# Mixing tiles beside the last convolution, and the first pair's blocks summed in other tiles

## The chip, the cores and the metric

The kernel runs on one core of one Trainium2 chip. The time is the device time of one execution in microseconds (us): the median of three runs. The profile is one further execution, recorded by the hardware profiler. A core has five engines with a queue of instructions each: PE (TensorE, matrix products; PEld is its loading of weights), DVE (VectorE), ACT (ScalarE), POOL (GpSimd) and SP (SyncE, which only starts transfers). Engines wait for one another by semaphores, and a wait holds everything behind it in the same queue. Results of PE stand in PSUM banks until ACT or DVE has read them.

## The reference

One layer over 128 context tokens and 512 latent tokens, model width 1024. One wide projection feeds two branches, a gated long convolution and an attention over a neighbourhood:

```python
h = x * (1 + scale) + shift
z = h @ w_in          # 4 x hyena, 4 x attention, 2 x mixing, 1024 columns each
v_h, x1, x0 = short_conv(z_hyena)
u = v_h * x1
y_h = (irfft(rfft(u) * rfft(filter)) + u * d_bias) * x0
y_a = neighbourhood_attention(q, k, v, cached k and v, bias)     # 16 heads
p_h = (y_h * silu(g_h)) @ w_bh
p_a = (y_a * silu(g_a)) @ w_ba
m_h, m_a = split(sigmoid(m))
x_new = layer_norm(ALPHA * x + gate * ((m_h * p_h + m_a * p_a) @ w_out))
```

The keys and values of the context tokens are outputs too. Everything is computed in float32 precision: a weight or a token matrix is split into a high and a low part, and three products (high by high, high by low, low by high) make one.

## The kernel before

**Tiles of the projection.** The 640 tokens lie as columns, in two halves of 320. The weights come from `wall`, a list of 128 x 1024 tiles; tile i makes 128 output channels: 32 to 39 are queries, 40 to 47 keys, 56 to 63 the attention's gates (`T_GA`), 64 to 71 the mixing of the hyena branch (`T_MH`). The tokens stand in `hH`, `hL` (high and low part) and for two of the eight blocks of model channels in `hHp`, `hLp`.

**Direct tiles.** `proj(i)` makes one tile as 8 blocks x 3 passes x 2 halves = 48 matmuls of 128 x 320 into two of the four PSUM banks of `ps_mm`, named mm<i>_0 and mm<i>_1. Its weights come from `wtile`: raw load, high part `wh` on ACT, low part `wl` on DVE, or with "dma" the negated high part to which GpSimd adds `wall` by an accumulating transfer.

**Pairs.** `pair_tile(p)` makes two tiles together with a Strassen-like scheme: seven products of 12 matmuls, so 84 for 96. `ORDER` lists their token operands: b11, b21, b22 are blocks of the tokens, t1 to t4 are sums of blocks, which were stored to DRAM (`tok_d`) and come back as tiles named t1_00 and so on. On the weights' side a pair p needs seven 128 x 512 blocks: a11 and a12 are the halves of the raw tile ra<p>, s3 and a22 those of rb<p>, and s2_<p> is a tile of its own. s2 and s3 have a part of the other tile added by accumulating transfers of GpSimd. `sum1` (DVE) adds s1 = s2 + a22. Each block is split into wb<7p+j> (`high` on ACT, `low` on DVE, four products ahead) and used by product j, whose bank is sp<p>_x. Each half of a product calls `tick()`, which runs what `later(fn, n)` has put off for n ticks: evictions, sums, steps of the attention.

**Stages.** A prologue, then four quarters in which direct tiles, the short convolution and the long convolution by Fourier matrices are woven together. The last quarter's long convolution (`long_conv(3)`, `long_conv_back(3)`) is woven with `hand_over()`, which makes the direct tiles of values 0, queries and keys 0, queries and keys 1. The end of the convolution is a chain over three engines: ACT and DVE split the spectrum (ph3_*, pl3_*), PE multiplies it into yb3_*, ACT evicts it (ye3, yep3), PE transposes it (yp3, y6, y7), DVE multiplies it into yu6 and yu7, and GpSimd stores these to `yu_d`. `first_gates()` then makes the two gate tiles 56 and 57 directly, and converts the first blocks of pair 0. `scratch()` copies half of `hHp`, `hLp` into the first blocks of `hH`, `hL`, in whose second halves nothing is needed any more, so that the old tiles become eviction space (`spare_hHp`, `spare_hLp`). Then come eight heads; `HEADS` gives each its pairs (h gates of the hyena branch, m mixing, a gates of the attention, q queries and keys of a head), and `attend(j)` weaves in the attention of head j: `tiled(i)` makes scores and softmax steps, among them scalings on GpSimd (`scaled`), `turned(i)` the transposes and the product with the values. Last come w_bh, w_ba, w_out and the layer norm.

**What sets the order.** PE, DVE and ACT run in written order in the quarters and the heads:

```python
with tc.manual_schedule(engines={PE, DVE, Activation}):     # written out at line 1351
    for _ in first_gates():
```

SP and GpSimd are ordered by a scheduler, except for loads pinned by `pinned[0]`. Tiles are taken from pools: a new tile waits for the last use of the one in its slot. `yhp` has 9 rows named "yh", in which x0 of the convolution, yu6, yu7 and some token sums stand.

Of the kernel before, what the change touches and what calls it, by code (L numbers as in the profile page):

```python
# [45 lines left out]
def tile_hyena_natten_step(ctx: ExitStack, tc: tile.TileContext, a, o):  # L46
# [802 lines left out]
    def hand_over():  # L849
# [6 lines left out]
        out["slots_r"] = left.enter_context(tc.tile_pool(name="slots_r", bufs=1))  # L856
        yield from queries(1)
        last_keys = keys(1)
        yield next(last_keys)
        wraw(T_GA)  # L860
        wraw(T_GA + 1)
        yield from last_keys
        early[T_GA] = wtile(T_GA, "dma")

    def first_gates():
        early[T_GA + 1] = wtile(T_GA + 1)
        yield from gate_a(0)
        for g in range(AHEAD - 1):
            if g == 1:
                sum1(0)  # L870
            high(g)
            low(g)
        yield from gate_a(1)
# [242 lines left out]
    def operand(name):  # L1116
# [3 lines left out]
        if name == "b11":  # L1120
# [13 lines left out]
    def load_pair(p):  # L1134
        if p < len(pairs):
            load_a(p)
            load_b(p)
# [3 lines left out]
    def load_b(p):  # L1141
        i0, i1 = pairs[p]
        wall = a["wall"]
        ra = raws.pop(("a", p))
        rb = sp.tile([P, 1024], F32, tag="rb", bufs=2, name=f"rb{p}")
        s2 = sp.tile([P, 512], F32, tag="s", bufs=3, name=f"s2_{p}")[:]
        load_to(rb[:], wall[i1])
        load_to(s2, wall[i0][:, :512])
        a11, a12, s3, a22 = (r[:, 512 * h : 512 * h + 512] for r in (ra, rb) for h in range(2))
        nc.gpsimd.dma_start(s2, wall[i1][:, :512], accum_op=ALU.add)  # L1150
        nc.gpsimd.dma_start(s3, wall[i1][:, 512:], accum_op=ALU.add)  # L1151
        sums_[p] = [a11, None, s2, s3, a12, a22, None]
# [36 lines left out]
    def pair_tile(p, use):  # L1189
# [16 lines left out]
        for j in range(7):  # L1206
# [3 lines left out]
            dst, x = ps["xyvzxvz"[j]], operand(ORDER[j])  # L1210
# [72 lines left out]
    HEADS = ("h0 m0", "q2 h1 m1", "q3 m2 a2", "q4 h2 m3", "q5 m4 a4", "q6 h3 m5", "q7 a6", "m6 m7")  # L1283
# [13 lines left out]
    raws["a", 0] = slot(1, "v", "ra0")  # L1297
    load_to(raws["a", 0][:, :1024], a["wall"][pairs[0][0]])
    load_b(0)
    load_sums(1, SUMS[:2])  # L1300
    biases[0] = [bias_tile(h) for h in range(2)]
    load_sums(1, SUMS[2:3])
    load_sums(0, SUMS[3:])
    load_sums(1, SUMS[3:])
    pinned[0] = True
    load_pair(1)
# [44 lines left out]
    with tc.manual_schedule(engines={mybir.EngineType.PE, mybir.EngineType.DVE, mybir.EngineType.Activation}):  # L1351
        for _ in first_gates():
            pass
        scratch()
        for j in range(8):
            side, n_main, n_side = attend(j), N_PAIR * len(HEADS[j].split()), N_ATT if j < 7 else N_ATT + 3
            done = taken = 0
            for _ in mains(j):
                done += 1
                while taken * n_main < done * n_side:  # L1360
# [308 lines left out]
```

## Time and profile before

| | |
|---|---|
| median of 3 runs | 916.91 us (916.83 to 917.48) |
| profiled execution, its own time | 916.55 us |
| its span from first to last instruction | 914.8 us |
| granted TensorE clock, mean | 0.982 |
| PE busy | 877.8 us, 96% |
| DVE, ACT, POOL busy | 636.2, 449.5 and 186.0 us |
| moved by DMA | 168.56 MB |

The profile names an instruction by engine, line, operation and its tiles (out<-in). A releaser behind "<-" is what ended the idle time before it, by the semaphores. Times in the text are microseconds from the start of the span. The conversion of the weights for mm57 begins at 356.5, and the first transposes of attention inside pair 1 at 417.3: between these lies what the change rewrites.

### The profile page before, as it was taken

To read this page: it belongs to the slowest core of one execution; us is meant where nothing else is said; L and a number is where in the kernel's file an instruction comes from. 1 tells how busy PE (TensorE), PEld (TensorE's weight loads), DVE (VectorE), ACT (ScalarE), POOL (GpSimd) and SP (SyncE) were. 2 spreads that over 40 slices of the span, in tenths; PEclk is the share of its full clock that TensorE was granted. 3 is DMA by queue.
4 is the path that set the end of the run, shared out by engine and by line. 5 is a ranking of instruction groups with operands and counts; after the bars stand their busy time and mean duration, and the time that the engine had idled before them with its cause. 6 is when DMAs were issued, how large, how long until landed. Compare 5 with 4: busy or idle time off the path is not lost. (4 is left out here: it accounts for less than half of the span.)

```text
span 914.8 us, 17154 instructions
## 1 busy us (share of the span) xinstructions
PE 877.8 (96%) x6476; PEld 846.3 (93%) x6476; DVE 636.2 (70%) x1216; ACT 449.5 (49%) x955; POOL 186.0 (20%) x215
## 2 busy tenths in 40 slices
PE   8999999999899999669999999999999999999995
PEld 7799999999899999559999999999999999999884
DVE  4896675993785656628777677868777577667566
ACT  4485555645555443416666565656566632233200
POOL 0020111211100100144444334333435200000000
PEclk9999999999999999888999999999999999999998
DMA  8975676876556762896676767676654576446232
GB/s 335 403 194 133 144 169 149 222 174 155 123 115 161 193 158 50 281 311 202 166 224 175 205 165 218 179 209 163 197 148 122 183 276 236 170 149 212 101 110 89
DMA packets 72367, 168.56 MB, mean 184 GB/s; under 512 B 10684, under 2 KB 28860, under 8 KB 72285
## 3 DMA queue, kind: packets, MB, share of 16 engines
q1 hardware_dynamic: 53180, 123.06, 40.2%
q0 software_dynamic: 13488, 38.80, 21.9%
q10 hardware_dynamic: 5616, 5.61, 1.8%
q8 instruction: 51, 0.84, 0.4%
q14 instruction: 32, 0.25, 0.1%
HBM read 142.80 MB, written 23.99 MB: 182 GB/s over the span
## 5 line engine op out<-in xcount | busy, mean ns | idle before, releaser
L1214 PE MATMUL sp<-t,wb 128*128 128x320 f32 x1008 | 160.3, 313 | 0.2
L1214 PEld LDWEIGHTS sp<-t,wb 128*128 128x128 f32 x1008 | 151.9, 190 | 0.9 <-issue 0.9
L1214 PE MATMUL sp<-hH,wb 128*128 128x320 f32 x504 | 124.6, 318 | 10.5 <-DVE spare_hHp L1202 6.9
L1214 PEld LDWEIGHTS sp<-hH,wb 128*128 128x128 f32 x504 | 88.7, 192 | 13.7 <-ACT wb L1167 7.1
L182 PE MATMUL mm<-hH,wh 128*128 128x320 f32 x336 | 85.0, 318 | 10.9 <-DVE kl L836 5.5
L182 PE MATMUL mm<-hL,wh 128*128 128x320 f32 x336 | 83.1, 316 | 0.4 <-DVE hL L329 0.4
L182 PE MATMUL mm<-hH,wl 128*128 128x320 f32 x336 | 82.6, 315 | 0.2 <-DVE wl L102 0.2
L1214 PE MATMUL sp<-hL,wb 128*128 128x320 f32 x252 | 79.5, 315 | 0.6 <-DMA hL<-hLp 0.6
L162 POOL DMA_DIRECT2D wl<-wall x33 | 28.8, 872 | 226.9 <-ACT wl L161 208.0
L182 PEld LDWEIGHTS mm<-hH,wh 128*128 128x128 f32 x336 | 58.3, 192 | 13.6 <-DVE kl L836 6.1
L1167 ACT ACTIVATE wb<-s 128x512 fp32r<-128x512 f32 x63 | 39.8, 632 | 54.6 <-DVE s L1157 23.2
L163 ACT ACTIVATE wh<-raw 128x1024 fp32r<-128x1024 f32 x33 | 35.1, 1064 | 59.6 <-PE mm L182 44.5
L1175 DVE TENSOR_TENSOR wb<-s,wb 128x512 fp32r<-128x512 f32 x63 | 44.9, 714 | 25.9 <-ACT wb L1167 25.7
L182 PEld LDWEIGHTS mm<-hL,wh 128*128 128x128 f32 x336 | 58.3, 192 | 1.5 <-DVE hL L329 1.2
L182 PEld LDWEIGHTS mm<-hH,wl 128*128 128x128 f32 x336 | 58.5, 193 | 0.9 <-DVE wl L102 0.6
L994 POOL TENSOR_SCALAR p<-p,sm 128x384 f32<-128x384 f32 x32 | 47.1, 1481 | 31.7 <-DVE sm L992 17.5
L994 POOL TENSOR_SCALAR edge<-edge,sm 128x320 f32<-128x320 f32 x32 | 38.0, 1196 | 69.9 <-DVE sm L992 69.9
L1214 PEld LDWEIGHTS sp<-hL,wb 128*128 128x128 f32 x252 | 48.5, 192 | 1.1 <-DMA hL<-hLp 1.0
L1488 PE MATMUL out<-woh,yhs 128*128 128x512 f32 (+1 forms) x176 | 45.7, 373 | 0.0
L182 PE MATMUL mm<-yhs,wh 128*128 128x320 f32 x224 | 42.0, 309 | 0.0
L1151 POOL DMA_DIRECT2D rb<-wall x21 | 18.4, 875 | 107.0 <-DMA rb<-wall 87.1
L1202 DVE TENSOR_TENSOR spare_hHp<-sp,yu 128x320 f32<-128x320 f32 x63 | 30.3, 482 | 11.5 <-PE sp L1214 11.0
(404 smaller groups left out, 2260.6 us busy)
## 6 DMA issues: line engine op xcount, KB each, us to landing
raw<-wall SPq DMA_DIRECT2D x54, 512.0 KB, 3.7
wl<-wall POOLq DMA_DIRECT2D x33, 512.0 KB, 6.2
rb<-wall SPq DMA_DIRECT2D x21, 512.0 KB, 4.9
ra<-wall SPq DMA_DIRECT2D x21, 512.0 KB, 4.0
ada<-wada SPq DMA_DIRECT2D x16, 512.0 KB, 7.5
tm<-bias SPq DMA_DIRECT2D x16, 512.0 KB, 7.7
s<-wall SPq DMA_DIRECT2D x21, 256.0 KB, 4.1
rb<-wall POOLq DMA_DIRECT2D x21, 256.0 KB, 4.1
```

Source lines behind the costliest of these rows:

```text
L162: nc.gpsimd.dma_start(wl, a["wall"][i], accum_op=ALU.add)
L163: nc.scalar.activation(wh, raw[:], AF.Copy)
L182: nc.tensor.matmul(ps[hf][:, :HALF], wt[k], x[:, hf * HALF : (hf + 1) * HALF], start=(i == 0 and k == 0), stop=(i == lead[2] and k == NK - ...
L994: nc.gpsimd.tensor_scalar_mul(pv, pv, sm[:, 2, c : c + 1])
L1151: nc.gpsimd.dma_start(s3, wall[i1][:, 512:], accum_op=ALU.add)
L1167: nc.scalar.activation(made[g][:, 0], sums_[g // 7][g % 7], AF.Copy)
L1175: nc.vector.tensor_tensor(made[g][:, 1], sums_[g // 7][g % 7], f(made[g][:, 0]), op=ALU.subtract)
L1202: nc.vector.tensor_tensor(c, dst, c if j == 3 else ps["u"], op=ALU.add)
L1214: nc.tensor.matmul(dst, wk, x(xi, k), start=j < 4 and k == 0 and i == 0, stop=k == 3 and i == 2, skip_group_check=True,)
L1488: ins = nc.tensor.matmul(dst, m[k][:, c0 : c0 + P], w[:, c : c + n], start=(first and k == 0), stop=(last and k == 5), skip_group_check=True,)
```

## The change

1. In `hand_over()` the direct tiles of head 1's queries and keys go out. In their place `mix_tile(0)` and `mix_tile(1)` make mixing tiles 64 and 65 directly: 48 matmuls each, two halves of tanh on ACT into a row of `yhp` (mx0, mx1), one store by SP to `mh_d`.
2. Pair 0 was the gate pair h0 and pair 1 the mixing pair m0. Now pair 0 is q1, head 1's queries and keys, pair 1 is h0, and there is no m0. The number of pairs and of direct tiles is the same.
3. Pair 0 reads block b11 from the four token tiles where they are (`operand(name, p)`); from pair 1 on it is read from the copy that `scratch()` makes.
4. `first_blocks()` loads and sums pair 0's blocks in other tiles, earlier in the program: rb0 in two tiles of the pool `slots_q`, s2_0 in a row of `yhp`.
5. The load of rb is split in two halves for every pair, and the accumulating transfers of later pairs are put off by five ticks, or, for pair 1, written ahead of the heads.
6. The low part of gate tile 57's weights is made by "dma".
7. GpSimd and SP run in written order in the heads as well.
8. In head 0 the attention is put back by 8 of the 28 steps of its pairs.
9. The pool `slots_r` is opened after the hand-over, and the loads of sums, biases and pair 1 are written in another order.

On PE, around the end of the last convolution, the rows before were these (mm56 and mm57 are the gate tiles):

```order
L172 MATMUL yb3_1_3965<-ph3_3_3976,dftL_102 128x256
L182 MATMUL mm56_0_4360<-hH_85,wl56_4309 128x320
L182 MATMUL mm56_1_4361<-hH_85,wl56_4309 128x320
L170 MATMUL yb3_2_3999<-ph3_4_4000,dftH_101 128x256
L171 MATMUL yb3_2_3999<-pl3_4_4001,dftH_101 128x256
L172 MATMUL yb3_2_3999<-ph3_4_4000,dftL_102 128x256
L170 MATMUL yb3_2_3999<-ph3_4_4000,dftH_101 128x256
L171 MATMUL yb3_2_3999<-pl3_4_4001,dftH_101 128x256
L172 MATMUL yb3_2_3999<-ph3_4_4000,dftL_102 128x256
L625 MATMUL yp3_4033<-pack2_380,yep3_3924 128x128 x2
L635 MATMUL y6_4038<-pack2_380,ye3_3923 128x128 x4
L635 MATMUL y7_4072<-pack2_380,ye3_3923 128x128 x4
```

And now, where the same transposes end:

```order
L170 MATMUL yb3_2_3999<-ph3_4_4000,dftH_101 128x256
L171 MATMUL yb3_2_3999<-pl3_4_4001,dftH_101 128x256
L172 MATMUL yb3_2_3999<-ph3_4_4000,dftL_102 128x256
L170 MATMUL yb3_2_3999<-ph3_4_4000,dftH_101 128x256
L171 MATMUL yb3_2_3999<-pl3_4_4001,dftH_101 128x256
L172 MATMUL yb3_2_3999<-ph3_4_4000,dftL_102 128x256
L625 MATMUL yp3_4033<-pack2_380,yep3_3924 128x128 x2
L635 MATMUL y6_4038<-pack2_380,ye3_3923 128x128 x4
L635 MATMUL y7_4072<-pack2_380,ye3_3923 128x128 x4
L182 MATMUL mm56_0_4340<-hH_85,wh56_4283 128x320
L182 MATMUL mm56_1_4341<-hH_85,wh56_4283 128x320
L182 MATMUL mm56_0_4340<-hL_87,wh56_4283 128x320
```

The convolution's matmuls stood inside mm56, and behind the transposes came mm57; now all thirty of them and the transposes stand in one block between the last matmul of mixing tile 65 and the first of mm56.

ACT evicts these banks. Before, at the same place (k1 and kp1 are head 1's keys, sg0 the first gate):

```order
L621 ACTIVATE ye3_3923<-yb3_0_3925 128x512
L101 ACTIVATE ph3_4_4000<-X3_3531 128x512
L621 ACTIVATE ye3_3923<-yb3_1_3965 128x512
L621 ACTIVATE yep3_3924<-yb3_2_3999 128x256
L826 ACTIVATE k1_4290<-mm41_0_4236 128x64
L826 ACTIVATE k1_4290<-mm41_0_4236 128x128 x2
L829 ACTIVATE kp1_4295<-mm41_0_4236 128x128
L832 ACTIVATE k1_4290<-ck1_4227 128x2x128
L826 ACTIVATE k1_4290<-mm41_1_4237 128x64
L826 ACTIVATE k1_4290<-mm41_1_4237 128x2x128
L499 ACT_TABLE_LOAD
L499 ACTIVATE sg0_4359<-mm56_0_4360 128x320
```

Now (mx0 and mx1 are the rows of the mixing tiles):

```order
L101 ACTIVATE ph3_3_3976<-W3_3705 128x512
L101 ACTIVATE ph3_4_4000<-X3_3531 128x512
L621 ACTIVATE ye3_3923<-yb3_1_3965 128x512
L621 ACTIVATE yep3_3924<-yb3_2_3999 128x256
L870 ACT_TABLE_LOAD
L870 ACTIVATE mx0_4157<-mm64_0_4165 128x320
L870 ACTIVATE mx0_4157<-mm64_1_4166 128x320
L870 ACTIVATE mx1_4218<-mm65_0_4226 128x320
L870 ACTIVATE mx1_4218<-mm65_1_4227 128x320
L499 ACTIVATE sg0_4339<-mm56_0_4340 128x320
```

The evictions of the key tile mm41 behind the convolution are replaced by those of both mixing tiles, and mx0's row is the one that x0 of yu7 has just left.

On GpSimd, behind the memsets of the attention's edge tiles, before (edge, p0 and pp0 are scaled scores of attention):

```order
L900 MEMSET edge31_4113 128x64
L994 ISA
L994 TENSOR_SCALAR edge00_4107<-edge00_4107,sm0_4525 128x320
L994 TENSOR_SCALAR edge01_4109<-edge01_4109,sm0_4525 128x320
L994 TENSOR_SCALAR p0_0_1_4526<-p0_0_1_4526,sm0_4525 128x384
L994 TENSOR_SCALAR p0_1_1_4527<-p0_1_1_4527,sm0_4525 128x384
L996 TENSOR_SCALAR pp0_4528<-pp0_4528,sm0_4525 128x128 x2
L1151 DMA rb1_4347<-wall 128x512
L1150 DMA s2_1_4348<-wall 128x512
L1151 DMA rb2_4615<-wall 128x512
L1150 DMA s2_2_4616<-wall 128x512
```

And now:

```order
L908 MEMSET edge31_4113 128x64
L1167 DMA s2_1_4317<-wall 128x512
L1168 DMA rb1_4316<-wall 128x512
L1167 DMA s2_0_4295<-wall 128x512
L1167 DMA s2_2_4546<-wall 128x512
L1168 DMA rb2_4545<-wall 128x512
L1002 ISA
L1002 TENSOR_SCALAR edge00_4107<-edge00_4107,sm0_4583 128x320
L1002 TENSOR_SCALAR edge01_4109<-edge01_4109,sm0_4583 128x320
L1002 TENSOR_SCALAR p0_0_1_4584<-p0_0_1_4584,sm0_4583 128x384
L1002 TENSOR_SCALAR p0_1_1_4585<-p0_1_1_4585,sm0_4583 128x384
L1004 TENSOR_SCALAR pp0_4586<-pp0_4586,sm0_4583 128x128 x2
```

The accumulating transfers of pairs 1 and 2 stood behind the scalings and now stand ahead of them, together with that of pair 0's s2.

On SP, near the mixing stores, now:

```order
L871 DMA mh_d_77<-mx0_4157 128x640
L63 DMA t3_10_4310<-tok_d_81 128x640
L63 DMA t3_11_4312<-tok_d_81 128x640
L63 DMA ra1_4314<-wall 128x1024
L871 DMA mh_d_77<-mx1_4218 128x640
L63 DMA rb1_4316<-wall 128x512 x2
L63 DMA s2_1_4317<-wall 128x512
L63 DMA s2_0_4295<-wall 128x512
L63 DMA t1_10_4321<-tok_d_81 128x640
```

The load of pair 0's s2_0 stands behind the stores of both mixing rows and behind the loads of pair 1's blocks; before, it stood ahead of the token sums t2.

```diff
--- before.py
+++ after.py
@@ -853,17 +853,25 @@
         out["slots_l"] = left.enter_context(tc.tile_pool(name="slots_l", bufs=1))
         out["slots_q"] = left.enter_context(tc.tile_pool(name="slots_q", bufs=1))
         yield from chain(values(0), queries(0), keys(0))
-        out["slots_r"] = left.enter_context(tc.tile_pool(name="slots_r", bufs=1))
-        yield from queries(1)
-        last_keys = keys(1)
-        yield next(last_keys)
-        wraw(T_GA)
-        wraw(T_GA + 1)
-        yield from last_keys
-        early[T_GA] = wtile(T_GA, "dma")
+        yield from mix_tile(0)
+        last_mix = mix_tile(1)
+        yield next(last_mix)
+        for i in range(2):
+            wraw(T_GA + i)
+        yield from last_mix
+        for i in range(2):
+            early[T_GA + i] = wtile(T_GA + i, "dma")
+        load_a(0)
+        first_blocks()
+
+    def mix_tile(n):
+        th = row(yhp, "yh", f"mx{n}")
+        for hf, p in enumerate((yield from proj(T_MH + n, eng="dma"))):
+            nc.scalar.activation(th[:, CS[hf]], p[:, :HALF], AF.Tanh, scale=0.5)
+        nc.sync.dma_start(mh_d[n], th[:])
+        yield
 
     def first_gates():
-        early[T_GA + 1] = wtile(T_GA + 1)
         yield from gate_a(0)
         for g in range(AHEAD - 1):
             if g == 1:
@@ -1113,11 +1121,11 @@
         yield
 
 
-    def operand(name):
+    def operand(name, p):
         if name in tok:
             return lambda i, k: tok[name][i][k // 2][:, HALF * (k % 2) : HALF * (k % 2) + HALF]
         i0, j = int(name[1]) - 1, int(name[2]) - 1
-        if name == "b11":
+        if name == "b11" and p:
             return lambda i, k: (hH, hL)[i][:, k % 2, CS[k // 2]]
         return lambda i, k: (hH, hL)[i][:, 4 * i0 + k, CS[j]]
 
@@ -1134,22 +1142,32 @@
     def load_pair(p):
         if p < len(pairs):
             load_a(p)
-            load_b(p)
+            later(load_b(p), 5)
         else:
             wraw(T_BH + p - len(pairs))
 
     def load_b(p):
-        i0, i1 = pairs[p]
-        wall = a["wall"]
-        ra = raws.pop(("a", p))
         rb = sp.tile([P, 1024], F32, tag="rb", bufs=2, name=f"rb{p}")
         s2 = sp.tile([P, 512], F32, tag="s", bufs=3, name=f"s2_{p}")[:]
-        load_to(rb[:], wall[i1])
-        load_to(s2, wall[i0][:, :512])
-        a11, a12, s3, a22 = (r[:, 512 * h : 512 * h + 512] for r in (ra, rb) for h in range(2))
-        nc.gpsimd.dma_start(s2, wall[i1][:, :512], accum_op=ALU.add)
-        nc.gpsimd.dma_start(s3, wall[i1][:, 512:], accum_op=ALU.add)
-        sums_[p] = [a11, None, s2, s3, a12, a22, None]
+        return blocks(p, s2, rb[:, :512], rb[:, 512:])
+
+    def first_blocks():
+        s2 = row(yhp, "yh", "s2_0")[:, :512]
+        blocks(0, s2, *(out["slots_q"].tile([P, NT], F32, tag=t, name=f"rb0_{t}")[:, :512] for t in ("q", "ql")))()
+
+    def blocks(p, s2, s3, a22):
+        w0, w1 = (a["wall"][i] for i in pairs[p])
+        load_to(s3, w1[:, :512])
+        load_to(a22, w1[:, 512:])
+        load_to(s2, w0[:, :512])
+        ra = raws.pop(("a", p))
+        sums_[p] = [ra[:, :512], None, s2, s3, ra[:, 512:], a22, None]
+
+        def summed():
+            nc.gpsimd.dma_start(s2, w1[:, :512], accum_op=ALU.add)
+            nc.gpsimd.dma_start(s3, w1[:, 512:], accum_op=ALU.add)
+
+        return summed
 
     def sum1(p):
         s_ = sums_[p]
@@ -1207,7 +1225,7 @@
             g = 7 * p + j
             if j < 4:
                 ps["xyvz"[j]] = acc(f"sp{p}_{j}")[:, :HALF]
-            dst, x = ps["xyvzxvz"[j]], operand(ORDER[j])
+            dst, x = ps["xyvzxvz"[j]], operand(ORDER[j], p)
             for k in range(4):
                 wh, wl = (made[g][:, i, P * k : P * k + P] for i in range(2))
                 for i, (wk, xi) in enumerate(((wh, 0), (wh, 1), (wl, 0))):
@@ -1280,7 +1298,7 @@
         return pair_tile(p, use)
 
     N_PAIR = 14
-    HEADS = ("h0 m0", "q2 h1 m1", "q3 m2 a2", "q4 h2 m3", "q5 m4 a4", "q6 h3 m5", "q7 a6", "m6 m7")
+    HEADS = ("q1 h0", "q2 h1 m1", "q3 m2 a2", "q4 h2 m3", "q5 m4 a4", "q6 h3 m5", "q7 a6", "m6 m7")
     MAKE = dict(a=gates_a, h=gates_h, q=queries_keys, m=mix)
 
     def tiles_of(item):
@@ -1294,16 +1312,16 @@
     pairs = [tiles_of(item) for item in items]
 
     weave(hand_over(), chain(long_conv(3), long_conv_back(3), attention_setup()), 4 * NK + N_VALUES, N_CONV + N_BACK + 1)
-    raws["a", 0] = slot(1, "v", "ra0")
-    load_to(raws["a", 0][:, :1024], a["wall"][pairs[0][0]])
-    load_b(0)
+    out["slots_r"] = left.enter_context(tc.tile_pool(name="slots_r", bufs=1))
+    pinned[0] = True
     load_sums(1, SUMS[:2])
-    biases[0] = [bias_tile(h) for h in range(2)]
+    load_a(1)
+    sums_of_second = load_b(1)
     load_sums(1, SUMS[2:3])
+    biases[0] = [bias_tile(0)]
     load_sums(0, SUMS[3:])
     load_sums(1, SUMS[3:])
-    pinned[0] = True
-    load_pair(1)
+    biases[0].append(bias_tile(1))
     pinned[0] = False
 
     def yh_home(i):
@@ -1348,16 +1366,19 @@
         for n in (2, 3):
             later(lambda n=n: yh_split(n), 6 + 2 * n)
 
-    with tc.manual_schedule(engines={mybir.EngineType.PE, mybir.EngineType.DVE, mybir.EngineType.Activation}):
+    engines = {getattr(mybir.EngineType, e) for e in ("PE", "DVE", "Activation", "Pool", "SP")}
+    with tc.manual_schedule(engines=engines):
         for _ in first_gates():
             pass
+        sums_of_second()
         scratch()
         for j in range(8):
-            side, n_main, n_side = attend(j), N_PAIR * len(HEADS[j].split()), N_ATT if j < 7 else N_ATT + 3
+            late = 8 if j == 0 else 0
+            side, n_main, n_side = attend(j), N_PAIR * len(HEADS[j].split()), {0: 3, 7: N_ATT + 3}.get(j, N_ATT)
             done = taken = 0
             for _ in mains(j):
                 done += 1
-                while taken * n_main < done * n_side:
+                while taken * (n_main - late) < (done - late) * n_side:
                     if next(side, StopIteration) is StopIteration:
                         break
                     taken += 1
```

## The prediction

> **What bounds the kernel now.** I read the page first: busy shares, then the strip in 40 slices (22.9 us each; PE is TensorE, and the figures are tenths of a slice that it was busy, below them the granted clock).
>
> ```profile
> span 914.8 us, 17154 instructions
> PE 877.8 (96%) x6476; PEld 846.3 (93%) x6476; DVE 636.2 (70%) x1216; ACT 449.5 (49%) x955; POOL 186.0 (20%) x215
> PE   8999999999899999669999999999999999999995
> PEclk9999999999999999888999999999999999999998
> ```
>
> TensorE is the bound nearly everywhere, so only its idle time and a lowered clock can be won. Both are found in one place, slices 17 to 19 (366 to 434 us), and the change rewrites that place. Next I read windows (start:end, length, busy time and count of PE, PEld, DVE, ACT, POOL, then clock, DMA share, GB/s); the first is the whole stretch from the first matmuls of gate tile mm56 to the point in pair 1 behind which nothing is held up any more.
>
> ```profile
> 356.57:417.31 60.74, 43.46 (x258) 40.76 (x257) 26.61 (x64) 21.49 (x53) 13.78 (x20) 0.83 0.75 239
> 365.00:376.00 11.00, 4.84 (x32) 3.83 (x31) 6.67 (x18) 4.18 (x11) 3.29 (x8) 0.87 0.62 185
> 386.00:394.00 8.00, 3.79 (x22) 2.95 (x21) 4.10 (x13) 1.80 (x6) 0.00 (x0) 0.76 1.04 373
> 405.00:412.00 7.00, 0.46 (x4) 0.20 (x2) 1.47 (x3) 0.63 (x1) 2.50 (x3) 0.90 0.95 150
> 440.00:480.00 40.00, 40.00 (x320) 39.00 (x321) 30.63 (x75) 23.57 (x56) 17.97 (x19) 1.00 0.67 190
> 376.00:377.00 1.00, 1.00 (x5) 1.00 (x5) 0.39 (x1) 0.90 (x3) 0.00 (x0) 0.50 0.76 211
> 380.00:381.00 1.00, 1.00 (x9) 1.00 (x8) 0.00 (x0) 0.52 (x1) 0.00 (x0) 1.00 1.12 376
> ```
>
> PE idles 60.74 - 43.46 = 17.3 us here, nearly all in three stalls (11.00 - 4.84 = 6.2 in the second window, then 4.2 and 6.5), and not at all from 440 to 480. After the first stall the clock is 0.50 at 376 and 1.00 at 380; it is a second cost. The list of waits names the releasers (sum, count, longest):
>
> ```profile
> PE mm L182 <- DVE kl L836: 5.5, 2, 5.2
> PE sp L1214 <- DMA hH<-hHp: 3.6, 1, 3.6
> PE sp L1214 <- DVE spare_hHp L1202: 6.9, 1, 6.9
> DVE s L1157 <- DMA s<-wall: 11.2, 1, 11.2
> ```
>
> Stall 1: mm57 needs the PSUM banks of head 1's keys, whose eviction stands behind the end of the long convolution. Stall 2: pair 0's first product reads the scratch copy of the tokens, still in flight. Stall 3: the eviction of a product's bank stands on VectorE behind pair 1's block sum, and that waits 11.2 us for an accumulating load.
>
> What the stretch costs at full pitch I take from these rows (start, length; x36 counts the matmuls):
>
> ```profile
> 419.58 5.48 PE L1214 MATMUL sp<-t,wb 128*128 128x320 f32 x36
> 360.04 0.28 PE L172 MATMUL yb<-ph,dftL 128*128 128x256 f32 x1
> 361.11 0.28 PE L172 MATMUL yb<-ph,dftL 128*128 128x256 f32 x1
> 368.29:369.60 1.31, 1.31 (x10) 1.07 (x10) 0.83 (x4) 0.00 (x0) 0.00 (x0) 1.00 0.55 78
> 385.56:387.12 1.56, 1.56 (x19) 1.25 (x18) 1.56 (x6) 0.88 (x2) 0.00 (x0) 1.00 1.02 405
> 400.53:401.74 1.21, 1.21 (x14) 1.02 (x13) 0.00 (x0) 0.00 (x0) 1.21 (x2) 1.00 1.15 414
> ```
>
> One 320-column matmul each 0.148 us (5.48 less the last one's tail of some 0.15, by 36); 186 of them stand between 356.57 and 417.31 (48 for each of mm56 and mm57, 84 of pair 0, 6 of pair 1, as the kernel is written): 27.5. Thirty convolution matmuls at 0.119 (nine steps in 1.07): 3.6. Ten transposes 1.3, attention scores 1.6 + 1.2. Sum 35.2. PE was busy 43.5, so the low clock took 8.3, or 2.8 per restart after each of three stalls. Lost in all: 17.3 + 8.3 = 25.6 us. That is the most the change can bring here.
>
> **The change, part by part.** *Tiles exchanged.* Two mixing tiles go where head 1's query and key tiles were, and those become pair 0 in place of the mixing pair m0. Direct tiles stay at 48 matmuls and pairs at 84, so PE's work is equal, and up to 356.57 it runs as before: 0. ACT does two tanh halves per tile instead of the key copies, VectorE loses the key low parts before mm56 and mm57: no PE time by itself.
>
> *Stall 1.* Convolution and transposes now run as one block behind the second mixing tile, ahead of gate tile mm56; before, they were spread inside mm56, which covered their ACT and VectorE steps. So cover is lost and the chain starts earlier. Its steps:
>
> ```profile
> 356.52 1.06 ACT L101 ACTIVATE wh<-raw 128x1024 fp32r<-128x1024 f32 x1 [2.33 <-PE mm L182]
> 365.55 0.63 ACT L101 ACTIVATE ph<-X 128x512 fp32r<-128x512 f32 x1 [3.12 <-PE yb L171]
> 366.21 0.69 DVE L102 TENSOR_TENSOR pl<-X,ph 128x512 fp32r<-128x512 f32 x1 [3.54 <-ACT ph L101]
> 366.38 0.60 ACT L621 ACTIVATE ye<-yb 128x512 f32<-128x512 f32 x1 [0.20 <-PE yb L172]
> 372.54 0.76 DVE L474 TENSOR_TENSOR yu<-x,u 128x64 f32<-128x64 f32 x2
> 376.14 0.77 ACT L499 ACTIVATE sg<-mm 128x320 f32<-128x320 f32 x2
> 368.29 0.44 PE L625 MATMUL yp<-pack,yep 128*128 128x128 f32 x2 [0.47 <-ACT yep L621]
> ```
>
> The weight conversion ends at 357.58 as before. Behind it ACT does ph3_1 (0.63), an eviction (0.60), ph3_3 and ph3_4 (0.63 each): 360.1; VectorE's low part (0.69, with handovers) ends at about 361.0, where before it ended at 366.21 + 0.69 = 366.90: 5.9 earlier. From there to the end of the last yu product took 373.30 - 366.90 = 6.4; so 367.4. The first tanh writes the row that this product read, so it starts there; one half takes about 0.43 (two in 0.77), with the handover 0.6: mm56 starts at 368.05. PE has done 3.6 + 1.3 since 356.57, so it loses 11.48 - 4.9 = 6.6, and one restart, 2.8. This stall stays.
>
> *Is the second mixing tile's tanh in time?* It reuses a row that the yu6 store reads. mm57 wants its banks at 368.05 + 7.1 + 2.8 = 378.0. The landings of stores and loads (KB each, median us):
>
> ```profile
> yu_d<-yu POOLq DMA_DIRECT2D x6, 320.0 KB, 4.0
> yu_d<-yu POOLq DMA_DIRECT2D x2, 320.0 KB, 10.5
> s<-wall SPq DMA_DIRECT2D x3, 256.0 KB, 5.3
> s<-wall POOLq DMA_DIRECT2D x3, 256.0 KB, 6.0
> s<-wall POOLq DMA_DIRECT2D x1, 256.0 KB, 8.9
> ```
>
> The store is issued at about 366.4 and lands after 4.0 (six in earlier quarters) to 10.5 (these two), thus 370.4 to 376.9; tanh 0.8 later; 377.7 at worst: 0.
>
> *Stall 2.* Pair 0's b11 now reads the four token tiles themselves, not the copy: -3.6, -0.6 for the low part, and its restart. The copy has until pair 1's b11, over 12 us after mm57: hidden by pair 0's 84 matmuls.
>
> *A new wait.* Product 1 of pair 0 needs s2_0, which is loaded into a row that yu7's store must leave, then accumulated on GpSimd, summed and split. The store is issued at 367.9; I take 5 for it, nearest the 4.0, because the two stores start where the DMA share was 0.62, not 1.04: 372.9. The load stands on SP behind the second mixing store (which waits for the tanh, 372.3) and three loads: issued 374.1, +5.3 = 379.4. Accumulate 0.6 and 6.0: 386.0; sum 0.69 and high part 0.63: 387.3; handovers 0.7: 388.0. PE gets there at 378.0 + 7.1 (mm57) + 1.8 (product 0, 12 matmuls) = 387.0. So the wait is 1.0 (bounds: 0, and 8.7 with the contended 10.5 and 8.9). A restart I don't add: the wait of 0.47 at 368.29 (last row above) left the clock at 1.00 in the window that begins with it.
>
> *Stall 3.* Its cause is GpSimd's order, read from three rows:
>
> ```profile
> 397.74 2.67 POOL L994 TENSOR_SCALAR edge<-edge,sm 128x320 f32<-128x320 f32 x2 [22.35 <-DVE sm L992]
> 404.60 1.16 POOL L1150 DMA_DIRECT2D s<-wall  x1
> 410.54 0.69 DVE L1157 TENSOR_TENSOR s<-s,rb 128x512 f32<-128x512 f32 x1 [11.18 <-DMA s<-wall]
> ```
>
> The accumulate was issued at 404.60 only because the scalings, waiting for softmax sums, stood ahead of it. Now pair 1's and 2's accumulates stand before them; they wait for loads issued by 375, so pair 1's are in by about 390, and its first sum is wanted some 10 us later. -6.9 and its restart, 2.8. What stands behind the accumulates now are the scalings of attention's first tile, whose scores were put back to product 4 of pair 0: 388.0 + four products (7.1) + 1.6 = 396.7. The softmax steps in between took 10.6 before (scores' end 387.12 to 397.74), with stall 2 inside, which held ACT's exponentials; without it I take 10.6 less 4.2 and the restart's 2.8, so 3.6, at most 10.6. Then scalings of 6.2 (397.74 to 403.97): 406.5. The transposes that read them stand behind two products of pair 0, four of pair 1 and the next scores: 396.7 + 10.7 + 1.2 = 408.6. Cost 0, covered by 2.1 us; at the upper end 413.5, 4.9 late, and a restart.
>
> *SP's queue* carries 23 more DMAs (393 for 370), mostly halves of the rb loads, and ACT's 4 fewer; one weight's low part more is made by accumulation on GpSimd (0.5 MB). In the stretch the loads of sums, biases, ra2, rb2 end just ahead of use: 0, up to 2.
>
> Sum: lost now 6.6 + 2.8 + 1.0 = 10.4; before 25.6; gain 15.2. The profiled execution took 916.55 us, so 901.4; the median of the runs, 916.91, stands 0.36 above it: **901.8**.
>
> [...]
>
> **Rivals.**
> 1. *The new wait is contended.* Stores and accumulates land as these two (10.5) and the slow one (8.9) did: s2_0 at 394.3, high part 395.6, PE waits 8.7 and restarts for 2.8: 901.4 - 1.0 + 11.5 + 0.4 = 912.3; with one of them slow, about 907. The scalings at their upper end give 901.8 + 4.9 + 2.8 = 909.5, a neighbour of this case. For it: DMA share 1.04 from 386 to 394, and loads for gates and pairs now crowd into 366 to 386. Against it: a share of 0.62 from 365 to 376, and the six earlier stores at 4.0. Chance 0.24, a third of it near 907, a third near 909.5.
>    [...]
> 2. *Slower: SP in written order.* In the steady part a load of SP may now stand behind the key store, which waits for ACT.
>
> ```profile
> SPq L63 <- DVE s L1161: 111.3, 20, 12.7
> SPq L830 <- ACT k L832: 44.2, 6, 7.4
> ```
>
>    These waits are there already, and cost PE nothing from 440 to 480. If written order makes VectorE wait as at stall 3, an 11.2 us wait there held PE 6.9; so from 4.3 us on PE is held, and a full case costs 6.9 + 2.8 = 9.7. There are seven such pairs of queries and keys: two cases (19.4) outweigh the gain of 15.2: 921. Chance 0.06.
> 3. *The stalls only move*: the scalings hold PE as long as stall 3 did (9.7) and the new wait is half contended: 901.8 + 9.7 + 5 = 916.5. Chance 0.03.
> 4. *Better than 898.5*: the chain block runs closer and mm56 starts 3 us earlier. Chance 0.04.
>
> **How the numbers follow.** The likeliest case, 0.63, gives 901.8; its own range is 898.5 (chain 1 us faster, no new wait, restart 1.7) to 905.5 (a 2 us late load or scaling that adds half a restart). The range goes to 898.0 and 912.5: it holds that case (0.63), rival 1 (0.24) and half of rival 4 (0.02), and leaves out rivals 2 and 3. A difference of 0.2% (1.8 us) is about what a measurement of this kernel can tell from none. Faster: 0.63 + 0.24 + 0.04 = 0.91; same 0.03 (rival 3); slower 0.06 (rival 2).
>
> **What would show it.** Stall 1: mm56 first waits for ACT's tanh mx0 and starts near 368. Stall 2: no PE wait on hH<-hHp. New wait: product 1 of pair 0 waits about 1 us for ACT wb or DVE s. Stall 3: no VectorE wait of over 4 us on s<-wall, accumulates issued before the scalings. Half clock once between 360 and 420, not three times; PE full from 420 to 880. Wrong would be: a second half clock near 388 (rival 1), PE idle after 420 behind SP (rival 2), or a wait of PE on the scaled tiles near 408.

## The result, and the profile after

The changed kernel takes 905.21 us (median of 4 runs, 904.71 to 907.25), the kernel before 916.87 in the runs beside it: a ratio of 0.988, 95% interval 0.986 to 0.990. That is 1.2% faster, 3.4 us slower than forecast, and inside the range. The profiled execution took 904.75 us. Its page (busy shares, PE's strip, the clock under it; a slice is 22.6 us):

```profile
span 903.0 us, 17145 instructions
PE 872.3 (97%) x6476; PEld 841.3 (93%) x6476; DVE 637.4 (71%) x1215; ACT 450.0 (50%) x956; POOL 189.9 (21%) x216
PE   8999999999999999879999999999999999999995
PEclk9999999999999999889999999999999999999998
```

The dip is shallower and has not gone. The list of waits from 340 to 420 shows two stalls of PE where there were three, and the wait behind the second:

```profile
PE sp L1232 <- ACT wb L1185: 5.1, 1, 5.1
PE mm L182 <- ACT mx L870: 4.2, 1, 4.2
...
DVE s L1175 <- DMA s<-wall: 10.6, 1, 10.6
```

The first stands ahead of mm56 and waits for the tanh of the first mixing tile, as forecast. The second stands ahead of product 1 of pair 0 and waits for its block sum: the new wait of the prediction, five times as long. In order of time (start, length; x counts; in brackets the idle time ahead and its releaser):

```profile
354.15 1.06 ACT L163 ACTIVATE wh<-raw 128x1024 fp32r<-128x1024 f32 x1 [3.28 <-PE mm L182]
365.53 0.96 PE L182 MATMUL mm<-hH,wh 128*128 128x320 f32 x2 [4.19 <-ACT mx L870]
370.38 1.20 SPq L63 DMA_DIRECT2D s<-wall  x2
377.68 1.55 POOL L1167 DMA_DIRECT2D s<-wall  x1
387.26 0.69 DVE L1175 TENSOR_TENSOR s<-s,rb_ql 128x512 f32<-128x512 f32 x1 [10.56 <-DMA s<-wall]
388.67 7.88 PE L1232 MATMUL sp<-t,wb 128*128 128x320 f32 x36 [5.13 <-ACT wb L1185]
```

**A common start.** The conversion of the weights for mm57, the first row, began at 356.52 before and begins at 354.15 here, though both kernels do equal matmuls up to there. The windows of PE alone (length, busy, clock, DMA share, GB/s) show why, first before, then after:

```profile
0.00:20.00 20.00, 17.55 (x142) 0.91 0.87 325
240.00:350.00 110.00, 109.25 (x807) 0.98 0.63 152
```

```profile
0.00:20.00 20.00, 17.32 (x159) 1.00 0.87 326
240.00:350.00 110.00, 109.38 (x817) 1.00 0.68 160
```

A lowered clock ahead of the stretch shows in some executions of kernels of both kinds: 0.91 from 0 to 20 in before and a_rooms, 0.91 from 40 to 60 in a_sched, b_b11 and b_acc. Over all profiles of this document the conversion began between 354.1 and 356.9, in kernels made from the one before (354.3 to 356.5) as in those made from the changed one. So I count each run from that conversion to its span's end as well. Before: 914.8 - 356.5 = 558.3; after: 903.0 - 354.15 = 548.9. The change brought 9.4 us there; the other 2.4 of the difference between the two profiles (11.8) is the clock ahead.

### The profile page after: what moved, and what is told of

Same layout as the page of the kernel before. It is cut to its first block, busy times and chain, and to the rows that moved or that the text cites. A ratio compares the mean times of both kernels' runs of the same rounds, so it can differ in the third digit from the quotient of the medians.

```text
span 903.0 us, 17145 instructions
## 1 busy us (share of the span) xinstructions
PE 872.3 (97%) x6476; PEld 841.3 (93%) x6476; DVE 637.4 (71%) x1215; ACT 450.0 (50%) x956; POOL 189.9 (21%) x216
## 5 line engine op out<-in xcount | busy, mean ns | idle before, releaser
L1232 PE MATMUL sp<-hH,wb 128*128 128x320 f32 x500 | 121.1, 313 | 0.0
L1232 PEld LDWEIGHTS sp<-hH,wb 128*128 128x128 f32 x500 | 85.9, 188 | 2.8 <-issue 2.8
L1232 PE MATMUL sp<-hL,wb 128*128 128x320 f32 x250 | 77.3, 309 | 0.0
L1002 POOL TENSOR_SCALAR p<-p,sm 128x384 f32<-128x384 f32 x32 | 50.3, 1667 | 22.0 <-DVE sm L1000 15.8
L1002 POOL TENSOR_SCALAR edge<-edge,sm 128x320 f32<-128x320 f32 x32 | 41.7, 1405 | 52.1 <-DVE sm L1000 52.1
L1220 DVE TENSOR_TENSOR spare_hHp<-sp,yu 128x320 f32<-128x320 f32 x63 | 30.5, 483 | 16.8 <-PE sp L1232 11.5
L1509 PEld LDWEIGHTS out<-woh,yhs 128*128 128x128 f32 x176 | 32.0, 188 | 6.2
```

The lines of the kernel that those rows point to most:

```text
L1002: nc.gpsimd.tensor_scalar_mul(pv, pv, sm[:, 2, c : c + 1])
L1220: nc.vector.tensor_tensor(c, dst, c if j == 3 else ps["u"], op=ALU.add)
L1232: nc.tensor.matmul(dst, wk, x(xi, k), start=j < 4 and k == 0 and i == 0, stop=k == 3 and i == 2, skip_group_check=True,)
L1509: ins = nc.tensor.matmul(dst, m[k][:, c0 : c0 + P], w[:, c : c + n], start=(first and k == 0), stop=(last and k == 5), skip_group_check=True,)
```

## The experiments

"Stretch" is that time from the conversion to the end of the span, of each run's profile; the ratio is against the kernel before in the runs beside it (for the experiments its median was 915.0 to 915.7).

| run | median us | ratio, 95% interval | stretch | against before |
|---|---|---|---|---|
| before | 916.87 | | 558.3 | |
| after | 905.21 | 0.988 (0.986-0.990) | 548.9 | -9.4 |
| a_s2room | 897.26 | 0.981 (0.980-0.983) | 541.5 | -16.8 |
| a_rooms | 900.08 | 0.984 (0.982-0.985) | 541.6 | -16.7 |
| a_copy | 905.27 | 0.990 (0.988-0.992) | 549.1 | -9.2 |
| a_sched | 905.84 | 0.991 (0.989-0.994) | 549.3 | -9.0 |
| a_late0 | 904.95 | 0.990 (0.988-0.992) | 548.7 | -9.6 |
| b_b11 | 914.61 | 1.000 (0.998-1.001) | 557.7 | -0.6 |
| b_acc | 912.41 | 0.997 (0.996-0.998) | 556.4 | -1.9 |
| b_b11acc | 912.71 | 0.998 (0.996-0.999) | 556.9 | -1.4 |
| b_early | 910.17 | 0.994 (0.993-0.996) | 553.2 | -5.1 |
| b_earlyb11 | 907.42 | 0.991 (0.989-0.994) | 550.1 | -8.2 |
| a_best | 900.55 | 0.984 (0.982-0.985) | 543.3 | -15.0 |
| a_best2 | 898.07 | 0.983 (0.980-0.985) | 541.8 | -16.5 |

Runs named a_ start from the changed kernel, runs named b_ from the one before. A stretch is that of one execution, and its far end varies too: the last 500 matmuls and what follows them took between 101.0 and 103.2 us in these profiles. Differences of less than a microsecond between stretches tell nothing.

**The new wait taken away (a_s2room).** `slots_r` is opened ahead of the mixing tiles, and s2_0 goes into the room of head 1's values:

```diff
+        out["slots_r"] = left.enter_context(tc.tile_pool(name="slots_r", bufs=1))
         yield from mix_tile(0)
...
-        s2 = row(yhp, "yh", "s2_0")[:, :512]
+        s2 = slot(1, "v", "s2_0")[:, :512]
```

> The changed kernel with pair 0's s2_0 loaded into the room of head 1's values (slots_r opened before the mixing tiles) and no longer into a convolution row; the mixing rows stay. Theory (the wait of 5.1 us before product 1 of pair 0 is the late load of s2_0, its accumulate behind two others, and costs its length and a clock restart of some 2.8): the load is issued right behind the last yu product at about 365 instead of 371, landed, accumulated and split by 379 to 381, before PE wants it at 383.5; the wait and one of the two half clocks go, 905.2 - 7.9 = 897.3. Rival (the transfers are saturated from 367 to 383 and set the pace): s2_0 is earlier, but t2, t3 or pair 1's blocks are late in its place, a wait of 3 us or more stays before pair 0 is done, 902 or more. First stall: unchanged by both, mm56 at 365.5.

Measured 897.26, as the theory had it. GpSimd and VectorE, then windows of the whole core:

```profile
369.42 0.90 POOL L1168 DMA_DIRECT2D s<-wall  x1 [3.15 <-DMA s<-wall]
378.34 0.69 DVE L1176 TENSOR_TENSOR s<-s,rb_ql 128x512 f32<-128x512 f32 x1 [1.59 <-DMA s<-wall]
374.00:384.00 10.00, 10.00 (x70) 10.00 (x69) 5.33 (x10) 4.62 (x11) 1.78 (x2) 1.00 1.05 380
384.00:394.00 10.00, 9.95 (x75) 9.27 (x74) 4.82 (x10) 2.55 (x6) 0.00 (x0) 1.00 1.06 340
```

The accumulate is issued 8.3 us earlier and takes 8.9, nearly as long as in the changed kernel (9.5), though it is now the first of the three on GpSimd and not the last. The sum is there ahead of PE, which hardly stops from 374 to 394 (0.05 us), and the second half clock is gone. So the wait for s2_0 cost 7.4 of the stretch: 5.1 and its restart. What helped is the earlier issue, not a faster transfer.

**The first stall too (a_rooms).** The mixing rows go into the room of head 1's keys:

```diff
-        th = row(yhp, "yh", f"mx{n}")
+        th = slot(1, ("k", "kl")[n], f"mx{n}")[:, :NT]
```

> The changed kernel with s2_0 in the room of head 1's values and both mixing rows in the room of its keys. Theory: the first stall is the wait of tanh mx0 for the last product of the convolution, which reads the row that mx0 takes; in a room of its own the tanh follows the eviction yep and a table load, some 361.5 to 362, and mm56 starts 3 us earlier, at 362 instead of 365.5, perhaps without a half clock; then pair 0 reaches product 1 at 379.5 to 380 with s2_0 ready between 379 and 381. Time 905.2 - 7.9 - 3 = 894, with no first restart 891.5. Rival 1: the earlier start only meets s2_0 or the token sums earlier, so that a wait of 3 us or more comes back before pair 0's end: no better than the run with s2_0 alone, about 897. Rival 2: tanh stays behind something else on ACT until the convolution has ended: mm56 at 365, 897.

```profile
356.71 1.06 ACT L163 ACTIVATE wh<-raw 128x1024 fp32r<-128x1024 f32 x1 [3.27 <-PE mm L182]
367.66 1.28 ACT L871 ACT_TABLE_LOAD   x1 [5.13 <-DVE yu L474]
369.44 0.96 PE L182 MATMUL mm<-hH,wh 128*128 128x320 f32 x2 [5.55 <-ACT mx L871]
```

Rival 2: the tanh still waits for the last yu product, now ahead of its table load, which adds 1.3. The room of the keys is not free before the convolution ends; the profile before already showed this, where the eviction of head 1's keys into that room (ACT L826, 373.41) began behind the same product. The stretch, 541.6, equals that of a_s2room as far as a stretch can tell; the profiled execution is longer by its later start (356.71), and whether the other runs of the median are so too is not shown.

**Pair 0's b11 from the copy again (a_copy).**

```diff
-        if name == "b11" and p:
+        if name == "b11":
```

> The changed kernel with pair 0's b11 read from the copy again, as before the change. If what the direct read brought is the 4.2 us of stall 2 and its restart, 2.8, on its own: 905.2 + 7.0 = 912. Theory: in the changed kernel the copy, issued from 376.3 on, lands by 388, and PE would wait there from 382.5 to 388; behind it stands the wait for s2_0 until 388.7 anyhow, so that the two waits lie in the same time, and the loss is the six matmuls behind the copy at half clock, 1.6: 906.8, between 905.5 and 908.

Measured 905.27, just below the theory's range. PE's longest wait moves from the block to the copy and is no longer:

```profile
PE sp L1232 <- DMA hH<-hHp: 4.3, 1, 4.3
```

In the changed kernel the direct read brings nothing, because the wait for s2_0 lies over the same time. The loss of 1.6 that the theory put on the matmuls behind the copy did not show (the stretch is 0.2 longer).

**SP and GpSimd ordered by the scheduler (a_sched).**

```diff
-    engines = {getattr(mybir.EngineType, e) for e in ("PE", "DVE", "Activation", "Pool", "SP")}
+    engines = {getattr(mybir.EngineType, e) for e in ("PE", "DVE", "Activation")}
```

> The changed kernel with SP and GpSimd ordered by the scheduler again. GpSimd's accumulates of pairs 1 and 2 stay ahead of the scalings; SP's order differs (rb2, v1 and cv1 stand earlier, the sums t4 and the copies later). If the written order is what removed stall 3: 905.2 + 9.7 = 915. Theory: what removed it is that pair 1's loads are issued at 369 and its accumulates are written ahead of the heads, both of which stay: 905 within 2, with no wait of VectorE for pair 1's accumulate; a wait for t4 (product 5 of pair 0) of up to 2 us could add to it. In the steady part, no difference.

Measured 905.84, a stretch 0.4 longer, the waits as after (5.4 for the block, 4.2 ahead of mm56, 0.2 for an eviction). The written order by itself is worth nothing that these runs can tell.

**Head 0's attention not put back (a_late0).**

```diff
-            late = 8 if j == 0 else 0
+            late = 0
```

> The changed kernel with the attention of head 0 not put back (its scores again in product 0 of pair 0). Theory: the 1.6 us of scores then lie in front of the wait for s2_0 and fill it, -1.6; but GpSimd has the scalings ahead of pair 2's accumulates, whose sum then comes late at pair 1's end, as stall 3 did: +2 to +6 with a restart; 905 to 911. Rival: pair 2's accumulates are wanted so late that the scalings cost nothing: 903.6.

```profile
PE sp L1232 <- ACT wb L1185: 3.5, 1, 3.5
PE sp L1232 <- DVE spare_hHp L1220: 1.4, 1, 1.4
```

The first part of the theory shows: 1.6 are filled. The second does not: GpSimd issues pair 2's accumulates only at 405.7, behind the scalings, but PE never waits for their sum. The 1.4 are lost earlier, at product 5 of pair 0 (400.8): VectorE begins the eviction that PE waits for at 400.27, after the first softmax steps of head 0. Sum: no difference.

**Only b11 in place, on the kernel before (b_b11).**

```diff
-        if name == "b11":
+        if name == "b11" and p:
```

> The kernel before with one edit: pair 0's b11 is read from the token tiles themselves and not from the copy. Theory: stall 2 goes with its restart, 4.2 + 2.8: 916.9 - 7.0 = 909.9, and stall 3 stays about as long (pair 1's loads are issued at 391.6 as before, land at 397, and its accumulate some 6 to 7 later; PE arrives at it 7 earlier, the scalings too). Rival: stall 3 is set by those loads alone, and grows by what stall 2 gave: 915 to 917.

Measured 914.61, a ratio of 1.000: the rival. Waits, then GpSimd, then SP:

```profile
PE sp L1214 <- DVE spare_hHp L1202: 12.8, 1, 12.8
```

```profile
397.61 0.94 POOL L1151 DMA_DIRECT2D rb<-wall  x1 [1.68 <-DMA rb<-wall]
```

```profile
389.79 0.43 SPq L63 DMA_DIRECT2D rb<-wall  x1
```

Stall 2 is gone and stall 3 has grown from 6.9 to 12.8. The scalings, done earlier, no longer hold the accumulate: it waits for its own load, which SP issued at 389.8 behind the scratch copies.

**Only the accumulates ahead of the scalings (b_acc), and both (b_b11acc).** GpSimd is in written order, and pair 1's accumulates are written ahead of the heads:

```diff
+        sums_of_second()
         scratch()
```

> The kernel before with GpSimd in written order and pair 1's accumulates written ahead of the heads, so ahead of the scalings. Theory: the accumulate is issued when its load has landed, about 397.5 instead of 404.6, the sum s1 runs at 404 to 405 instead of 410.5, stall 3 falls from 6.9 to under 1 and loses its restart: 916.9 - 6.2 - 2.8 = 908. Rival: the transfers of that time (share 1.0 from 386 to 405) make the accumulate land late wherever it is issued: 914 or more.

> The kernel before with both edits: b11 in place, accumulates ahead of the scalings. If the two stalls add: 916.9 - 7.0 - 9.0 = 901. Theory: they don't, since pair 1's loads, issued at 391.6, bound the accumulate to 404 or so, and PE is there at 398.5: a wait of 5 and its restart stay, so 907 to 909. It would tell that the early loads of pair 1 are part of what the change brought.

```profile
398.09 0.90 POOL L1153 DMA_DIRECT2D s<-wall  x1 [24.10 <-DMA s<-wall]
```

```profile
PE sp L1218 <- DVE spare_hHp L1206: 4.6, 1, 4.6
```

```profile
406.70 0.69 DVE L1161 TENSOR_TENSOR s<-s,rb 128x512 f32<-128x512 f32 x1 [8.84 <-DMA s<-wall]
```

b_acc 912.41 (GpSimd, then PE's wait, then VectorE): the accumulate, first in the queue now, still waits for its load until 398.1, and takes 8.6 to the sum where it took 5.9 before (404.60 to 410.54). Stall 3 falls only to 4.6. b_b11acc 912.71, with one wait of 12.1: the two edits don't add, and bring less than expected.

**Pair 1's loads early (b_early, and b_earlyb11 with b11 in place).** As b_acc, and ra1, rb1 and s2_1 are loaded ahead of the token sums, the biases and the copies:

```diff
+    load_a(1)
+    sums_of_second = load_b(1)
     load_sums(1, SUMS[:2])
```

> The kernel before with pair 1's accumulates ahead of the scalings, as in the run b_acc, and besides pair 1's loads (ra1, rb1, s2_1) put ahead of the second token sums, the biases and the scratch copies on SP. Theory (stall 3 is the late load of pair 1's blocks, issued at 391.6 behind the copies, and not GpSimd's order): rb1 and s2_1 are issued near 369, their accumulates are in before 390, the sum s1 of pair 1 no longer waits, stall 3 goes with its restart: 915.0 - 6.9 - 2.4 = 905.7 beside 915.0 for the kernel before on this chip; stall 2 stays at 3 to 6. Rival: the three loads only move the lateness to the copies and to pair 0's own blocks: 911 or more.

> The same with pair 0's b11 read in place too. Theory: with stall 3's cause gone, stall 2's removal counts in full: b_early less 4.2 and a restart of 2 to 2.4, near 899, so that these two edits alone bring at least what the whole change brought. Rival: pair 0's blocks or the token sums t4 become the next wait, as s2_0 did in the changed kernel: 903 to 907.

PE's rows of b_early, then its wait on ACT:

```profile
386.94 0.63 PE L1218 MATMUL sp<-hH,wb 128*128 128x320 f32 x1 [3.52 <-ACT wb L1171]
395.07 0.64 PE L1218 MATMUL sp<-hH,wb 128*128 128x320 f32 x1 [3.27 <-DMA hH<-hHp]
```

```profile
ACT wb L1171 <- DMA ra<-wall: 10.8, 1, 10.8
```

Stall 3 is gone in both: no wait of PE behind these rows. What hid part of the gain is an effect of my edit: ra0, pair 0's own first block, lands late. SP issues it as long after the conversion as before (16.9 us: at 372.0, before at 373.4), but with the loads put ahead of it still under way it takes 14.2 us to land where it took 7.0, and product 0 waits 3.5 (3.7 in b_earlyb11). So b_early (910.17) gave 5.1 where 9.3 were expected, b_earlyb11 (907.42) 8.2: its rival, a wait for pair 0's own blocks, is what came. Between them the direct read of b11 is worth 3.1, where with late loads it was worth 0.6.

**The first stall once more (a_best).** a_s2room, and t1_00 and t1_01 are loaded behind the convolution, which frees rows for the mixing tiles:

```diff
-        load_sums(0, SUMS[:3])
+        load_sums(0, SUMS[:2])
...
+    load_sums(0, SUMS[2:3])
     load_sums(1, SUMS[2:3])
```

> The changed kernel with s2_0 in the room of head 1's values, and the two token sums t1_00 and t1_01 loaded behind the convolution instead of ahead of it, which hands mixing tile 64 a row that nothing of the convolution reads any more, and tile 65 that of yu6. Theory: tanh mx0 follows the eviction yep and the table load, at about 361.3 by the clock of the changed kernel's profile, mm56 starts at 362 instead of 365.5 and without a half clock; PE reaches product 1 of pair 0 at 378, the blocks are ready at 379.5 to 380: 3.5 us less than with s2_0 alone, 897.3 - 3.5 = 893.8, between 892 and 896. Rival: t1, now loaded when transfers are saturated, is late at product 3 by 2 us or more: 896 to 899.

```profile
362.04 0.74 PE L182 MATMUL mm<-hH,wh 128*128 128x320 f32 x2 [0.44 <-ACT mx L871]
393.17 3.54 PE L1233 MATMUL sp<-t,wb 128*128 128x320 f32 x12 [5.11 <-issue]
392.58 0.49 DVE L1221 TENSOR_TENSOR spare_hHp<-sp,yu 128x320 f32<-128x320 f32 x1 [8.47 <-DMA hH<-hHp]
```

The first stall is gone as forecast, with its half clock (from 362.6 to 370 two matmuls start every 0.29 us, as at full pitch). In its place VectorE waits 8.5 for the scratch copies, issued from 382.4 on, and PE waits 5.1: its row names no releaser, but it starts 0.1 after VectorE's eviction has ended (393.07). That is neither the theory nor the rival, and 900.55.

**The copies ahead of t4 (a_best2).**

```diff
         scratch()
+        load_sums(0, SUMS[3:])
+        load_sums(1, SUMS[3:])
+        biases[0].append(bias_tile(1))
```

> The run a_best with the scratch copies put on SP ahead of the four sums t4 and of the second bias. What a_best showed: mm56 at 362.0 with a wait of only 0.4, product 1 of pair 0 at 378.6, and then a wait of 5.1 behind VectorE's eviction into the scratch tile, which waited 8.5 for the copy out of that tile, issued at 382.4 to 384.5. Theory: issued some 4 us earlier, the copies land near 387, VectorE's wait falls from 8.5 to under 4, what PE can bear without idling (8.5 - 5.1 = 3.4), and the stall goes with its half clock: 900.5 - 5.1 - 2 = 893.4, between 892 and 896. Rival: the sums t4, now 2 us later, are wanted at product 5 (387.5) and are not there: a wait of 2 to 4 takes the place, 896 to 899, no better than 897.3 of the run with s2_0 alone.

```profile
390.00 0.38 PE L1233 MATMUL sp<-t,wb 128*128 128x320 f32 x1 [1.68 <-ACT k L826]
390.69 3.33 PE L1233 MATMUL sp<-t,wb 128*128 128x320 f32 x11 [0.31 <-DMA t<-tok_d]
```

```profile
366.00:376.00 10.00, 10.00 (x70) 10.00 (x70) 1.54 (x3) 1.28 (x3) 1.50 (x6) 1.00 1.01 311
376.00:386.00 10.00, 9.40 (x65) 8.68 (x63) 6.42 (x12) 4.85 (x10) 1.78 (x2) 1.00 1.05 373
386.00:396.00 10.00, 8.01 (x49) 6.90 (x46) 4.63 (x15) 3.36 (x11) 0.00 (x0) 0.83 1.06 371
```

The rival: 898.07, no better than a_s2room. PE stands for 2.0 us at product 5 and loses the clock again. The last 0.3 of it are named as t4. The first 1.7 are named after ACT's keys, which product 5 does not read; the first of the loads of t4 was issued at 381.90, 8.1 ahead of the row, and this run's loads of t took a median of 7.7 between 356 and 400, so I take t4 for the cause there too. The DMA share is 1.01 to 1.06 for thirty microseconds, and three orders of the same loads (a_s2room, a_best, a_best2) came out between 541.5 and 543.3. I take the transfers to be the limit of this stretch now; that is argued from the share, and no run with fewer bytes was made.

## Why the prediction was right, and where it was off

- **Stall 1: right.** Forecast 11.5 us from the conversion to mm56 (356.52 to 368.05); measured 11.4 (354.15 to 365.53).
- **The restart, 2.8: too large, and not one price.** From 365.53 to 381.62 PE ran the 96 matmuls of mm56 and mm57 in 16.1 us instead of 14.2: 1.9. Behind the second stall 36 matmuls took 7.88 instead of 5.48: 2.4. The second is nearer the price of 2.8. The restart of 1.7 at the range's lower end had no run behind it, and neither of the two profiles shows one; in its place stand these 1.9 and 2.4 (only the shorter half clock of a_best2, 3.4 us, comes to 3.4 / 2 = 1.7). What the size went with is shown in the last section.
- **The new wait, 1.0: the step that failed.** Its load was issued at 371 and PE's arrival came at 383.5, 29.4 after the conversion (forecast 30.5). But the accumulate, put at 0.6 and 6.0, took 9.5 (377.68 to 387.2) beside loads at full share. Its place as the last of three on GpSimd is not what made it slow: in a_s2room it was the first and took 8.9. Counted from the conversion the product began 34.5 us later and not 31.5. "A restart I don't add" fell with it: the sign that the prediction named for rival 1, a second half clock near 388, is there (0.50 from 388 to 389), and VectorE waits 10.6 on s<-wall, for pair 0's block and not for pair 1's. This is rival 1 with one slow transfer, priced at about 907: the profiled execution, put on the start of the profile before, is 904.75 + 2.4 = 907.1. The accumulate's place ahead of the scalings on GpSimd did not keep it short: from 376 to 388 the DMA share was 1.00, and it took those 9.5.
- **Stall 2: gone, but not worth its 7.0.** On the kernel before its removal went nearly whole into stall 3 (b_b11, 0.6 us left), and in the changed kernel it lies under the wait for s2_0 (a_copy). Stalls in a row were added in the sum as if each stood alone.
- **Stall 3: gone, for another reason than I gave.** "Its cause is GpSimd's order" holds for the row in the profile before, but with that order put right alone (b_acc) the accumulate still began only at 398.1, when its load was in, and then took 8.6 beside the others: 1.9 us gained of 9.7. The loads at 369 to 371 instead of 391 to 392, with the accumulates ahead of the scalings, are what removed it (b_early); no run had the early loads with the accumulates still behind the scalings, so what the order adds to them is not shown.
- **The scalings and the steady part: right.** PE had no wait from 390 on and was busy 460.0 of 460 us from 420 to 880; neither the scalings nor SP's written order (rival 2, a_sched) cost anything.
- The sum was 15.2; the stretch gave 9.4. The difference, 5.8, is the longer wait (4.1) and its restart (2.4), less the first restart's 0.9, within 0.2. The profiled execution came nearer to the forecast only because the clock ahead of the stretch was better by 2.4, which is luck. The likeliest case (0.63, one small wait and no second restart) is not what happened, though the median fell into its range of 898.5 to 905.5; what happened is the part of rival 1 near 907, a third of 0.24.

## What to carry to other kernels

When several stalls stand in a row, find for each what is late next before adding them up: take one away in thought and look at when the load behind the following one was issued, not only at what stood ahead of it in its queue. A load that must be followed by an accumulate, a sum and a split belongs early in the queue, into a tile that is free by then (a_s2room); whether a place with fewer other transfers would have shortened the accumulate itself was not tried. And compare two profiles from a point at which both have done the same work, since a lowered clock early on shifts what stands behind it (2.4 us between these two profiles).

## What the runs showed of the hardware

- In these runs an accumulating transfer of 256 KB took longer beside many other loads. In the changed kernel the last of three that were issued from 376.5 to 377.7 took 9.5 us (DMA share 1.00 and 301 GB/s from 376 to 388), and in a_s2room the first took 8.9 (0.82 and 281 GB/s from 364 to 374, 1.05 and 380 from 374 to 384). In the profile before, the one issued at 404.60 took 5.9 (0.95 and 150 GB/s from 405 to 412); over its whole span 21 into s had a median of 5.9 and 21 into rb one of 4.1.
- In a_best2 a half clock followed on some 2.0 us of standing (1.68 and 0.31, one matmul apart): the windows (PE, PEld, DVE, ACT, POOL, clock, DMA share, GB/s) show it from about 391.1 (a clock of 0.56 from 391 to 392), when work had already resumed. No half clock followed on the single waits of 0.44 at 362.04 in a_best (two matmuls every 0.29 us behind it) and of 0.47 at 368.29 in the profile before (a clock of 1.00 from 368.29 to 369.60).

```profile
390.00:391.00 1.00, 0.69 (x3) 0.46 (x4) 0.00 (x0) 0.45 (x2) 0.00 (x0) 1.00 1.04 417
391.00:392.00 1.00, 1.00 (x6) 0.91 (x4) 0.00 (x0) 0.00 (x0) 0.00 (x0) 0.56 1.05 415
```

- In the profiles before and after, the half clock lasted equally long at every stall, wherever work resumed in it. In the changed kernel it stood from 362.9 to 369.7 and from 386.8 to 393.6, 6.8 us each, as the mean clock of the windows below tells; in the profile before, windows of the same kind give 373.1 to 379.9, 390.1 to 397.0 and 410.6 to 417.5, also 6.8 each. In the changed kernel half of what was left of that time when PE started again is (369.7 - 365.5) / 2 = 2.1 and (393.6 - 388.7) / 2 = 2.5, beside the 1.9 and 2.4 that the matmuls lost. It was not so long in every run: in a_best2 it lasted 3.4 us (391.1 to 394.5, by clocks of 0.56 and 0.73 in the first and the last window).

```profile
362.00:363.00 1.00, 0.00 (x0) 0.00 (x0) 1.00 (x2) 0.00 (x0) 0.00 (x0) 0.94 0.76 302
369.00:370.00 1.00, 1.00 (x6) 1.00 (x6) 0.00 (x0) 0.00 (x0) 0.00 (x0) 0.65 1.00 261
386.00:387.00 1.00, 0.00 (x0) 0.00 (x0) 0.00 (x0) 0.00 (x0) 0.00 (x0) 0.89 1.01 311
393.00:394.00 1.00, 1.00 (x6) 1.00 (x6) 1.00 (x3) 0.29 (x1) 0.00 (x0) 0.70 1.31 336
```

- When the second stall of the changed kernel ended, the transfers had run dry (a DMA share of 0.03 from 388 to 389): SP issued nothing from 380.9 to 390.0, behind a load into s2_0's row that waited for the accumulate (6.3) and then for VectorE's split of the sum, its last reader (2.7).

```profile
388.00:389.00 1.00, 0.33 (x1) 0.33 (x2) 0.35 (x1) 1.00 (x2) 0.00 (x0) 0.50 0.03 9
```
